# The down projection of a gated feed-forward: eight of 22 tiles as seven block products, three groups of plain tiles around them

## The chip, the cores and the metric
The kernel runs on one core of one Trainium2 chip. A core has five engines with instruction streams of their own: TensorE (PE, matrix products into PSUM), VectorE (DVE), ScalarE (ACT), GpSimd (POOL) and SyncE (SP, which here only starts transfers); they meet through semaphores. Sixteen DMA engines move data between DRAM and the on-chip memory SBUF. The metric is the device time of one execution in microseconds (us); lower is better.

## The reference
A trunk of two layers over 1024 frames and 16 learned meta tokens, model width 1024. Each layer has a mixing half (gated linear attention beside softmax attention, one output projection, residual add) and a gated feed-forward half. Only the second matters here:

```python
def conv_ffn(x, w_up, conv_w, conv_b, w_down):
    h = x @ w_up                              # 1024 -> 2 * 2816
    hp = jnp.pad(h, ((0, 0), (CONV_W - 1, 0), (0, 0)))
    hc = conv_b
    for j in range(CONV_W):                   # causal, 3 taps
        hc = hc + hp[:, j:j + L] * conv_w[j]
    u, g = jnp.split(hc, 2, axis=-1)
    return (jax.nn.silu(g) * u) @ w_down      # 2816 -> 1024
...
        h = h + conv_ffn(rms_norm(h, ffn_norm[i]), w_up[i], conv_w[i], conv_b[i], w_down[i])
    return rms_norm(h, final_norm)[:, N_META:]
```

All is float32, and the output must agree with the reference to nearly that precision.

## The kernel before
Everything is stored transposed: a tile is 128 features (partitions) by up to 1040 tokens. The hidden width 2816 is NFF = 22 such "gated tiles", the model width KD = 8 tiles. A float32 product is made as three products of a rounded type: each operand is split into a rounded high part and the rounded remainder, and `mm3` (lines 212 to 218) accumulates high x high, low x high, high x low in PSUM. ACT makes high parts by a cast, DVE low parts by a subtraction; `split` (line 326) does it for activations, `weights` (line 169) for weights, which SP loads from DRAM into four rotating "raw" buffers.

The up stage (`ffn_up`) makes gated tile j from two output tiles, u and g. It takes them, the two halves of the inner dimension and the two halves of the tokens as a 2 x 2 by 2 x 2 block product and needs seven block products instead of eight (numbered 1 to 7; operands are sums and differences of blocks, several products share a PSUM bank and are taken out of it between them). `up_operand` (line 979) loads and combines the weights, `put` the activations, `evacuate` copies a bank out by ACT (line 1181) or adds it onto a tile by DVE (line 1180). After a tile's last product ACT and DVE apply the convolution (ACT line 1169, DVE line 1173 twice for each of u and g), SiLU and the gate product (line 1202), and POOL starts the write of the tile to `actd[j]` in DRAM (line 1203).

The down stage adds 22 gated tiles times their weights onto the residual. `FGROUPS` cuts the 22 into groups of 5, 5, 5, 4 and 3. `load_act` (line 1228 on) loads a gated tile from `actd` into a slot "st" and splits it into "ah" (ACT, line 330) and "al" (DVE, line 331). While the last up tile runs, the first ten gated tiles are loaded; when a group ends, the next but one is. The first four groups run in `down_tiles`: for each group, for each of the eight output tiles m, all token pieces (three in layer 0, 400, 384 and 256 columns; two of 512 in layer 1, which drops the meta tokens), and DVE adds the PSUM result onto the residual `hT[m]`, which is in SBUF since the start of the stage (line 1249). `stream` asks for the weights of one output tile ahead. The last three gated tiles go to `down_last`, which runs token piece by token piece and feeds the next norm as it goes.

The order of the work is made in two ways. PE's instructions in the feed-forward run as they are written (a manual schedule). On ACT, DVE, POOL and SP a scheduler of the framework orders them by what it expects of their durations, and each stream then runs in that fixed order: an instruction that waits holds up all behind it on its engine. SBUF tiles of 1040 columns are slots of one pool (`self.slots`): `get` takes a free one, `put` gives it back, and the next user of a slot waits for the former one's last reader or writer, transfers among them.

## Time and profile before
| | us |
|---|---|
| median of 3 runs | 2651.08 |
| lowest, highest | 2644.53, 2653.59 |
| the profiled execution | 2645.09 |
| its span, first to last instruction | 2643.3 |
| PE busy in the span | 2523.9 (95%) |
| DVE, ACT, POOL busy | 1759.9 (67%), 1240.1 (47%), 457.9 (17%) |
| mean granted PE clock | 0.987 of full |

The profile is one execution taken by the hardware profiler. Its page gives busy time by engine and the chain of work that ended last; the trace behind it can be asked for waits (who waited for whom), groups of like instructions with counts and mean durations, transfers with their time from issue to landing, timelines, and busy time by stretch of the span. "L217" is line 217 of that kernel; "out<-in" are the names of the tiles. The down stage of layer 0 runs from about 1072 us, that of layer 1 from about 2380 us to the end. A group's busy time counts an instruction from its start to its end; instructions of one engine overlap a little, so the distance between starts is shorter than the duration.

### The profile page before, as it was taken

The numbers are of one execution on the slowest core, as the hardware profiler recorded it, in microseconds if no ns is written. First come the engines' busy times: TensorE is split into PE (matmuls) and PEld (weight loads), VectorE is DVE, ScalarE is ACT, GpSimd is POOL, SyncE is SP. The second block draws the span as 40 slices with busy tenths as digits, with TensorE's granted clock in tenths as the row PEclk, the third lists the DMA queues.
The fourth block names the chain that finished last, engine by engine and source line by source line (L and its number), as shares of the span: only waits on it lengthen the run. The fifth ranks groups of instructions, "written<-read, shape, count | busy, mean of one in ns | idle before, by whom it ended". The sixth has DMA issues, their size and how long they took to land.

```text
span 2643.3 us, 46336 instructions
## 1 busy us (share of the span) xinstructions
PE 2523.9 (95%) x18102; PEld 2407.2 (91%) x18102; DVE 1759.9 (67%) x3484; ACT 1240.1 (47%) x2677; POOL 457.9 (17%) x596
## 2 busy tenths in 40 slices
PE   8999999897999999999999999998989999999997
PEld 7988898897999999999999888887889999998886
DVE  7655676759877777643665666666698767776335
ACT  6345665645544445421343565665455444453112
POOL 4033333333000000000201333332320000000002
PEclk9999999998999999999999999999999999999999
DMA  3222124341222222632312222142512222245222
GB/s 125 65 83 70 47 83 124 106 131 58 97 81 76 85 77 92 217 94 58 103 56 65 75 72 74 56 138 91 158 51 85 83 81 77 83 139 189 65 55 77
DMA packets 114476, 240.72 MB, mean 91 GB/s; under 512 B 14432, under 2 KB 36192, under 8 KB 114256
## 3 DMA queue, kind: packets, MB, share of 16 engines
q1 hardware_dynamic: 96000, 182.27, 22.7%
q0 software_dynamic: 16384, 53.18, 5.5%
q8 instruction: 142, 2.33, 0.4%
q10 hardware_dynamic: 1872, 2.31, 0.2%
q14 instruction: 78, 0.64, 0.1%
HBM read 174.01 MB, written 50.91 MB: 85 GB/s over the span
## 4 chain that ended last, share of the span: by engine, by line
PE 77%; DVE 13%; ACT 4%; issue 3%; DMA 2%; POOL 2%; DVEq 0%; SPq 0%; POOLq 0%; ACTq 0%
PE mm L216 12%; PE mm L217 12%; PE mm L218 12%; PE up L216 10%; PE up L217 10%; PE up L218 10%; PE av L706 2%; PE tr L688 2%; DVE S L655 1%; DVE x L1038 1%; PE wo L217 1%; PE wo L216 1%; PE wo L218 1%; DVE PT L331 1%; ACT P L667 1%
## 5 line engine op out<-in xcount | busy, mean ns | idle before, releaser
L216 PE MATMUL up<-x,hi 128*128 128x260 f32 (+1 forms) x2464 | 701.3, 285 | 22.7 <-DVE hu L1180 20.3
L217 PE MATMUL up<-x,lo 128*128 128x260 f32 (+1 forms) x2464 | 699.2, 284 | 0.0
L218 PE MATMUL up<-x,hi 128*128 128x260 f32 (+1 forms) x2464 | 698.5, 283 | 0.0
L216 PEld LDWEIGHTS up<-x,hi 128*128 128x128 f32 x2464 | 467.5, 190 | 24.4 <-DVE hu L1180 20.7
L217 PEld LDWEIGHTS up<-x,lo 128*128 128x128 f32 x2464 | 467.9, 190 | 0.1
L218 PEld LDWEIGHTS up<-x,hi 128*128 128x128 f32 x2464 | 467.8, 190 | 0.0
L216 PE MATMUL mm<-xh,hi 128*128 128x348 f32 (+4 forms) x1056 | 365.1, 346 | 0.0
L218 PE MATMUL mm<-xl,hi 128*128 128x348 f32 (+4 forms) x1056 | 340.9, 323 | 0.0
L217 PE MATMUL mm<-xh,lo 128*128 128x348 f32 (+4 forms) x1056 | 340.8, 323 | 0.0
L1014 DVE TENSOR_TENSOR lo<-raw,hi 128x512 fp32r<-128x512 f32 x308 | 212.9, 694 | 146.2 <-ACT hi L1013 146.2
L183 ACT CAST hi<-raw 128x512 fp32r<-128x512 f32 (+1 forms) x264 | 142.3, 543 | 329.8 <-PE mm L218 240.0
L217 PE MATMUL mm<-ah,lo 128*128 128x400 f32 (+1 forms) x760 | 266.4, 351 | 0.2 <-DVE lo L185 0.2
L218 PE MATMUL mm<-al,hi 128*128 128x400 f32 (+1 forms) x760 | 265.9, 350 | 0.0
L216 PE MATMUL mm<-ah,hi 128*128 128x400 f32 (+1 forms) x760 | 265.8, 350 | 0.0
L185 DVE TENSOR_TENSOR lo<-raw,hi 128x512 fp32r<-128x512 f32 (+1 forms) x196 | 120.7, 620 | 181.1 <-ACT hi L183 177.5
L1013 ACT CAST hi<-raw 128x512 fp32r<-128x512 f32 x308 | 190.3, 620 | 107.6 <-PE up L218 92.7
L216 PEld LDWEIGHTS mm<-xh,hi 128*128 128x128 f32 x1056 | 201.0, 190 | 6.0 <-issue 5.3
L217 PEld LDWEIGHTS mm<-xh,lo 128*128 128x128 f32 x1056 | 200.9, 190 | 0.4 <-issue 0.3
L218 PEld LDWEIGHTS mm<-xl,hi 128*128 128x128 f32 x1056 | 199.9, 189 | 0.4 <-issue 0.3
L1203 POOL DMA_DIRECT2D actd<-cv x44 | 23.4, 533 | 830.0 <-DVE cv L1202 830.0
L667 ACT ACTIVATE P<-S,m 116x460 f32<-116x460 f32 (+2 forms) x224 | 124.8, 561 | 76.9 <-DVE m L655 72.6
L331 DVE TENSOR_TENSOR PT<-tr,PT 116x464 fp32r<-116x464 f32 (+3 forms) x240 | 122.1, 516 | 55.8 <-ACT PT L330 54.1
(248 smaller groups left out, 5269.0 us busy)
## 6 DMA issues: line engine op xcount, KB each, us to landing
raw<-in_wm_dram SPq DMA_DIRECT2D x328, 256.0 KB, 2.6
raw<-in_wd_dram SPq DMA_DIRECT2D x64, 256.0 KB, 2.6
actd<-cv POOLq DMA_DIRECT2D x22, 520.0 KB, 2.9
st<-actd SPq DMA_DIRECT2D x22, 520.0 KB, 4.9
actd<-cv POOLq DMA_DIRECT2D x22, 512.0 KB, 3.0
st<-actd SPq DMA_DIRECT2D x22, 512.0 KB, 4.8
cb<-cd SPq DMA_DIRECT2D x16, 520.0 KB, 4.2
kA<-kA SPq DMA_DIRECT2D x24, 260.0 KB, 3.8
```

The lines of the kernel that those rows point to most:

```text
L183: nc.scalar.copy(hi[:, :n, :], raw[:, :n, :])
L185: eng.tensor_tensor(out=lo[:, :n, :], in0=raw[:, :n, :], in1=hi[:, :n, :].bitcast(F32), op=ALU.subtract)
L216: nc.tensor.matmul(ps, wh, xh[:, c0:c0 + n], start=first, stop=False, skip_group_check=more)
L217: nc.tensor.matmul(ps, wl, xh[:, c0:c0 + n], start=False, stop=False, skip_group_check=more)
L218: nc.tensor.matmul(ps, wh, xl[:, c0:c0 + n], start=False, stop=last, skip_group_check=more)
L331: nc.vector.tensor_tensor(out=lo, in0=src, in1=hi.bitcast(F32), op=ALU.subtract)
L655: nc.vector.tensor_tensor_reduce(out=S[:rows, :n], in0=S[:rows, :n], in1=cb[:rows, c0:k1], scale=1.0, scalar=(BIG if ci == 0 else m[:rows, ...
L667: nc.scalar.activation(P[:rows, :n], S[:rows, :n], AF.Exp, scale=-1.0, bias=m[:rows, nch - 1:nch], accum_out=(den if nch == 1 else d3[:row ...
L688: nc.tensor.transpose(tr[:w, j, :rows], P[:rows, o:o + w], id_)
L706: nc.tensor.matmul(av[:, a:width], w.rearrange("p a b -> p (a b)"), x, start=(t == 0 and i == 0), stop=(t == last and i == 1))
L1013: nc.scalar.copy(hi[:], src[:])
L1014: nc.vector.tensor_tensor(out=lo[:], in0=src[:], in1=hi[:].bitcast(F32), op=ALU.subtract)
```

## The change
The 22 gated tiles are cut anew: `GROUPS = (("n", 0, 3), ("s", 3, 8), ("r", 11, 4), ("r", 15, 4))` and the last three as before. Lines here are those of the changed kernel.

- Group "n" (tiles 0 to 2) is plain, but its eight results are not added to a residual in SBUF: ACT copies them from PSUM into a slot "do" (line 1414), and POOL starts an accumulating transfer that adds the slot onto `hm[m]`, the residual in DRAM (line 1416). The PSUM tiles are those of the up stage (p0 to p3, two banks each), in token halves of 520 columns (512 in layer 1), each in two pieces of 260 (256).
- Group "s" (tiles 3 to 10) is done by `down_blocks`: output tiles in four pairs, the eight tiles as two halves of four, tokens in two halves; 7 products of 4 inner tiles for each pair. The seven activation operands are made by `prepare` in two sets (inner tiles 0 and 1, then 2 and 3): loads of half tiles, four combinations on DVE and seven splits for each set. Weights are combined and split by `block_operand`, the up stage's function, now with its sources as parameters. Results are built in slots "du" and "dg" by ACT copies and DVE adds and go to `hm` by accumulating transfers too (lines 1348 and 1352).
- Groups "r" are plain and add onto `hT` in SBUF by DVE (line 1412); `hT` is loaded from `hm` only when the first of them begins (line 1393).
- `prepare` is a generator. It yields how many free slots its next step needs, and `pump(n, keep)` runs up to n steps if that many and `keep` more are free. It is called after each product of the last up tile (`tail`), after each plain output tile and within the blocks; `complete` runs what is still missing when a group begins.
- `fetch` asks for the weights of a plain output tile up to two tiles ahead; the first two of group "n" are asked for during the last up tile.

The core of the diff (the weights' functions only gain a parameter `nk`):

```diff
-FGROUPS = [(0, 5), (5, 5), (10, 5), (15, 4), (19, 3)]
+GROUPS, LAST = (("n", 0, 3), ("s", 3, 8), ("r", 11, 4), ("r", 15, 4)), (19, 3)
+HALVES, HALVES_LAST, HALVES_OUT = (0, 520, 520), (8, 524, 516), (16, 528, 512)
-    def down_tiles(self, lyr, hT, pp, o0, dchunks, acts):
...
+    def prepare(self, halves, acts, X):
+        for kind, g0, ng in GROUPS + (("r",) + LAST,):
+            if kind != "s":
+                for j in range(g0, g0 + ng):
+                    yield 3
+                    self.load_act(j, halves[0], acts)
+                continue
...
+                yield 2 + m
+                a0, a1 = load(g0, 0), load(g0, 1)
+                put(1, a0)
+                yield 2 + m
+                b0, b1 = load(g0 + nk, 0), load(g0 + nk, 1)
+                put(2, b0)
+                yield 1 + m
+                tt(a1, b1, a1, ALU.subtract)
+                t2 = get("t2")
+                tt(t2, a1, a0, ALU.add)
+                put(6, t2)
+                yield m
+                tt(a0, b1, t2, ALU.subtract)
+                put(5, a0)
+                s.put(a0)
+                yield m
+                put(7, a1)
+                s.put(a1)
+                yield m
+                tt(b0, b0, t2, ALU.subtract)
+                s.put(t2)
+                put(4, b0)
+                s.put(b0)
+                yield m
+                put(3, b1)
+                s.put(b1)
+    def pump(self, n, keep=3):
+        s = self.slots
+        while n and self.need + keep <= len([i for i in s.free if i not in s.lent]):
+            self.need = next(self.prep)
+            n -= 1
+    def down_blocks(self, lyr, g0, ng, X, pp, fw, halves, after):
...
+        seq = [(0, 1), (0, 2), (1, 1), (0, 6), (0, 5), (0, 7), (0, 4), (0, 3)]
+        for j in range(1, NP):
+            seq += [(j, 2), (j, 6), (j, 5), (j, 7)] + ([(j + 1, 1)] if j + 1 < NP else []) + [(j, 4), (j, 3)]
...
+            elif p == 7:
+                q["g"] = s.get(F32, "dg")
+                copy(q["g"][:, t1])
+                add(q["g"][:, t1], q["x"])
+            elif p == 4:
+                copy(q["g"][:, t0])
+                nc.gpsimd.dma_start(self.hm[2 * j + 1][:, o0:T], q["g"][:, o0:T], accum_op=ALU.add)
+                s.put(q["g"])
+            elif p == 3:
+                add(q["u"][:, t1], q["x"])
+                nc.gpsimd.dma_start(self.hm[2 * j][:, o0:T], q["u"][:, o0:T], accum_op=ALU.add)
+                s.put(q["u"])
...
+    def ffn_down(self, lyr, pp, fw, halves, acts, X, ids):
...
+            out = hT[m] if kind == "r" else s.get(F32, "do")
+            for h in range(2):
+                ps = pp.tile([128, 2, 512], F32, tag=f"p{(2 * m + h) % 4}", name="down", bufs=1)
+                for k in range(ng):
+                    for c in range(2):
+                        self.mm3(ps[:, c, :n], w[k], acts[g0 + k], halves[h] + c * n, n, k == 0, k == ng - 1)
+                x = two(out[:, halves[h]:halves[h] + W])
+                if kind == "r":
+                    nc.vector.tensor_tensor(out=x, in0=ps[:, :, :n], in1=x, op=ALU.add)
+                else:
+                    nc.scalar.copy(x, ps[:, :, :n])
+            if kind == "n":
+                nc.gpsimd.dma_start(self.hm[m][:, o0:T], out[:, o0:T], accum_op=ALU.add)
+                s.put(out)
...
+        def tail(p):
+            self.pump(2 if p == 1 else 1)
+            if p in (5, 7):
+                fetch(parts[0])
-            acts, early = {}, {1: 2, 6: 2, 2: 1, 7: 2, 5: 1, 4: 1, 3: 1}
-            def during_last(p):
-                for _ in range(early[p]):
-                    self.load_act(len(acts), o0, acts)
```

More of the change, by code (lines that the diff above doesn't have):

```diff
@@ L32 @@
 CH_OUT = [(16, 512), (528, 256), (784, 256)]
-CH_DOWN = [(16, 512), (528, 512)]
 CTILES = [(0, 4), (4, 7), (7, 9)]
@@ L46 @@
 V_FIN = DEPTH * NV
-FGROUPS = [(0, 5), (5, 5), (10, 5), (15, 4), (19, 3)]
-HALVES, HALVES_LAST = (0, 520, 520), (8, 524, 516)
+GROUPS, LAST = (("n", 0, 3), ("s", 3, 8), ("r", 11, 4), ("r", 15, 4)), (19, 3)
+HALVES, HALVES_LAST, HALVES_OUT = (0, 520, 520), (8, 524, 516), (16, 528, 512)
 AHEAD = 4
@@ L979, in up_operand, with block_operand @@
     def up_operand(self, lyr, j, p, fw, raws, odd):
-        nc = self.nc
         if j == 2 and p in (1, 2):
             src = fw.tile([128, 4, 128], F32, tag="raw2", name="raw2")
-            nc.sync.dma_start(src[:], self.wm[lyr, M_UP + 4][:, 4 * p - 4:4 * p, :])
+            self.nc.sync.dma_start(src[:], self.wm[lyr, M_UP + 4][:, 4 * p - 4:4 * p, :])
             return self.up_split(src, fw, odd)
+        return self.block_operand(self.wm[lyr, M_UP + 2 * j], self.wm[lyr, M_UP + 2 * j + 1], 4, j, p, fw, raws, odd)
+    def block_operand(self, u, g, nk, j, p, fw, raws, odd):
+        nc = self.nc
         if j not in raws:
-            u, g = self.wm[lyr, M_UP + 2 * j], self.wm[lyr, M_UP + 2 * j + 1]
             q = raws[j] = {}
-            for name, src, k0, own in (("A11", u, 0, True), ("A21", g, 0, False), ("A22", g, 4, False), ("A12", u, 4, True)):
+            for name, src, k0, own in (("A11", u, 0, True), ("A21", g, 0, False), ("A22", g, nk, False), ("A12", u, nk, True)):
                 q[name] = self.wp.tile([128, 4, 128], F32, tag="raw", name="raw", bufs=4) if own else \
                     fw.tile([128, 4, 128], F32, tag="raw2", name="raw2")
-                nc.sync.dma_start(q[name][:], src[:, k0:k0 + 4, :])
+                nc.sync.dma_start(q[name][:, :nk, :], src[:, k0:k0 + nk, :])
         q = raws[j]
@@ L996, in combine @@
                 q[out] = fw.tile([128, 4, 128], F32, tag="raw2", name="raw2")
-            nc.vector.tensor_tensor(out=q[out][:], in0=q[a][:], in1=q[b][:], op=op)
+            nc.vector.tensor_tensor(out=q[out][:, :nk, :], in0=q[a][:, :nk, :], in1=q[b][:, :nk, :], op=op)
         if p == 6:
@@ L1005, in up_operand, with up_split @@
         src = q[{1: "A11", 2: "A12", 3: "A12", 4: "A22", 5: "S1", 6: "S2", 7: "A21"}[p]]
-        return self.up_split(src, fw, odd)
-    def up_split(self, src, fw, odd):
+        return self.up_split(src, fw, odd, nk)
+    def up_split(self, src, fw, odd, nk=4):
         nc = self.nc
@@ L1012, in up_split @@
         lo = pool.tile([128, 4, 128], F32R, tag="lo" + x, name="lo", bufs=3)
-        nc.scalar.copy(hi[:], src[:])
-        nc.vector.tensor_tensor(out=lo[:], in0=src[:], in1=hi[:].bitcast(F32), op=ALU.subtract)
-        return [(hi[:, k, :], lo[:, k, :]) for k in range(4)]
+        nc.scalar.copy(hi[:, :nk, :], src[:, :nk, :])
+        nc.vector.tensor_tensor(out=lo[:, :nk, :], in0=src[:, :nk, :], in1=hi[:, :nk, :].bitcast(F32), op=ALU.subtract)
+        return [(hi[:, k, :], lo[:, k, :]) for k in range(nk)]
     def ffn_up(self, lyr, mix, hT, pp, fw, halves, o0, during_last):
@@ L1238, in load_act, with load, put, tt @@
         acts[j] = (ah, al)
-    def down_tiles(self, lyr, hT, pp, o0, dchunks, acts):
+    def prepare(self, halves, acts, X):
         nc, s = self.nc, self.slots
-        def down(i, m):
-            g0, ng = FGROUPS[i]
-            def f(w):
-                def ev(ps, c0, n):
-                    h = hT[m][:, c0:c0 + n]
-                    nc.vector.tensor_tensor(out=h, in0=ps, in1=h, op=ALU.add)
-                self.dense3(pp, w, [acts[j] for j in range(g0, g0 + ng)], dchunks, ev)
-                if m == KD - 1:
-                    for j in range(g0, g0 + ng):
-                        s.put(*acts.pop(j))
-                    if i + 2 < len(FGROUPS):
-                        a, b = FGROUPS[i + 2]
-                        for j in range(a, a + b):
-                            self.load_act(j, o0, acts)
-            return (self.wd[lyr, m][:, g0:g0 + ng, :], f)
-        return [down(i, m) for i in range(len(FGROUPS) - 1) for m in range(KD)]
+        W = halves[2]
+        for kind, g0, ng in GROUPS + (("r",) + LAST,):
[4 more added lines that the diff above has]
+                continue
+            nk = ng // 2
+            for k0 in range(0, nk, 2):
+                m = min(2, nk - k0)
+                get = lambda name, dt=F32: s.get(dt, name, (128, 2, 520))
+                def load(j, h):
+                    t = get("st")
+                    for i in range(m):
+                        c = halves[h]
+                        nc.sync.dma_start(t[:, i, :W], self.actd[j + k0 + i][:, c:c + W])
+                    return t
+                def put(p, src):
+                    hi = get(f"x{p}", F32R)
+                    lo = get(f"x{p}", F32R) if m == 2 else hi
+                    h, l = (hi[:, :m, :W], lo[:, :m, :W]) if m == 2 else (hi[:, 0:1, :W], hi[:, 1:2, :W])
+                    self.split(h, l, src[:, :m, :W])
+                    X[g0][p].append(([hi, lo] if m == 2 else [hi], h, l))
+                def tt(out, a, b, op):
+                    nc.vector.tensor_tensor(out=out[:, :m, :W], in0=a[:, :m, :W], in1=b[:, :m, :W], op=op)
+                yield 2 + m
[24 more added lines that the diff above has]
+                s.put(b1)
+        yield 99
@@ new lines, in pump, with ensure, evacuate, run @@
+    def pump(self, n, keep=3):
[4 more added lines that the diff above has]
+    def down_blocks(self, lyr, g0, ng, X, pp, fw, halves, after):
+        nc, s = self.nc, self.slots
+        nk, o0, W = ng // 2, halves[0], halves[2]
+        n = W // 2
+        t0, t1 = (slice(c, c + W) for c in halves[:2])
+        two = lambda ap: ap.rearrange("p (a b) -> p a b", b=n)
+        NP = KD // 2
+        seq = [(0, 1), (0, 2), (1, 1), (0, 6), (0, 5), (0, 7), (0, 4), (0, 3)]
+        for j in range(1, NP):
+            seq += [(j, 2), (j, 6), (j, 5), (j, 7)] + ([(j + 1, 1)] if j + 1 < NP else []) + [(j, 4), (j, 3)]
+        raws, ops, st = {}, [], {}
+        wd = lambda m: self.wd[lyr, m][:, g0:g0 + ng, :]
+        def ensure(i):
+            while len(ops) < min(i + 1, len(seq)):
+                j, p = seq[len(ops)]
+                ops.append(self.block_operand(wd(2 * j), wd(2 * j + 1), nk, j, p, fw, raws, len(ops) % 2))
+        def evacuate(j, p):
+            q = st[j]
+            add = lambda out, ps: nc.vector.tensor_tensor(out=two(out), in0=ps[:, :, :n], in1=two(out), op=ALU.add)
+            copy = lambda out: nc.scalar.copy(two(out), q["a"][:, :, :n])
+            if p == 1:
+                q["u"] = s.get(F32, "du")
+                copy(q["u"][:, t0])
+            elif p == 2:
+                add(q["u"][:, t0], q["y"])
+            elif p == 6:
+                copy(q["u"][:, t1])
+            elif p == 7:
[10 more added lines that the diff above has]
+                s.put(q["u"])
+                del st[j]
+        def run():
+            for i, (j, p) in enumerate(seq):
+                ensure(i + AHEAD)
+                q = st.setdefault(j, {})
+                bank, begins = {2: "y", 5: "x", 3: "x"}.get(p, "a"), p in (1, 2, 5)
+                if begins:
+                    place = {1: j % 2, 2: 3, 5: 2}[p]
+                    q[bank] = pp.tile([128, 2, 512], F32, tag=f"p{place}", name="down", bufs=1)
+                ps, w = q[bank], ops[i]
+                ops[i] = None
+                for k in range(nk):
+                    _, hi, lo = X[p][k // 2]
+                    for c in range(2):
+                        self.mm3(ps[:, c, :n], w[k], (hi[:, k % 2, :], lo[:, k % 2, :]), c * n, n,
+                                 begins and k == 0, k == nk - 1, not begins)
+                evacuate(j, p)
+                if j == NP - 1:
+                    for held, _, _ in X.pop(p):
+                        s.put(*held)
+                    if len(ops) == len(seq):
+                        after()
+                    self.pump(1)
+                elif j and p == 5:
+                    self.pump(1, 4)
+        return ensure, run
@@ new lines, in ffn_down, with load_residual, complete, plain @@
+    def ffn_down(self, lyr, pp, fw, halves, acts, X, ids):
+        nc, s = self.nc, self.slots
+        o0, W = halves[0], halves[2]
+        n = W // 2
+        two = lambda ap: ap.rearrange("p (a b) -> p a b", b=n)
+        hT, ahead = [], []
+        def load_residual():
+            for k in range(KD):
+                hT.append(s.get(F32, f"h{k}", first=ids))
+                nc.sync.dma_start(hT[k][:, o0:T], self.hm[k][:, o0:T])
+        def complete(done):
+            while not done():
+                self.need = next(self.prep)
+        def plain(kind, g0, ng, m, w):
+            if m == 0:
+                complete(lambda: all(j in acts for j in range(g0, g0 + ng)))
+                if kind == "r" and not hT:
+                    load_residual()
+            out = hT[m] if kind == "r" else s.get(F32, "do")
+            for h in range(2):
+                ps = pp.tile([128, 2, 512], F32, tag=f"p{(2 * m + h) % 4}", name="down", bufs=1)
+                for k in range(ng):
+                    for c in range(2):
+                        self.mm3(ps[:, c, :n], w[k], acts[g0 + k], halves[h] + c * n, n, k == 0, k == ng - 1)
[7 more added lines that the diff above has]
+                s.put(out)
+            if m == KD - 1:
+                for j in range(g0, g0 + ng):
+                    s.put(*acts.pop(j))
+            self.pump(2)
+        parts = []
+        for kind, g0, ng in GROUPS:
+            if kind == "s":
+                parts.append((g0, ng))
+                continue
+            if not parts or not isinstance(parts[-1], list):
+                parts.append([])
+            parts[-1] += [(kind, g0, ng, m) for m in range(KD)]
+        def fetch(tiles):
+            if len(ahead) < len(tiles):
+                _, g0, ng, m = tiles[len(ahead)]
+                ahead.append(self.weights(self.wd[lyr, m][:, g0:g0 + ng, :]))
+        def run():
+            blocks = None
+            for i, part in enumerate(parts):
+                nxt = parts[i + 1] if i + 1 < len(parts) else None
+                if not isinstance(part, list):
+                    g0, ng = part
+                    complete(lambda: all(len(x) == (ng // 2 + 1) // 2 for x in X[g0].values()))
+                    blocks[1]()
+                    continue
+                if nxt:
+                    then = parts[i + 2] if i + 2 < len(parts) else []
+                    blocks = self.down_blocks(lyr, *nxt, X[nxt[0]], pp, fw, halves,
+                                              lambda t=then: len(ahead) < 2 and fetch(t))
+                for k, t in enumerate(part):
+                    for _ in range(2):
+                        if len(ahead) < k + 3:
+                            fetch(part)
+                    if nxt and k >= len(part) - 2:
+                        blocks[0](2 * (k - len(part) + 2) + 1)
+                    plain(*t, ahead[k])
+                ahead.clear()
+            if not hT:
+                load_residual()
+            complete(lambda: all(j in acts for j in range(LAST[0], sum(LAST))))
+            return hT
+        def tail(p):
+            self.pump(2 if p == 1 else 1)
+            if p in (5, 7):
+                fetch(parts[0])
+        return tail, run
@@ L1261, in down_last @@
     def down_last(self, lyr, hT, pp, dchunks, acts, at_end, es):
         nc, s = self.nc, self.slots
-        g0, ng = FGROUPS[-1]
+        g0, ng = LAST
         w, held = [], []
@@ L1346, in run @@
             dch = CH_OUT if last else CH
-            acts, early = {}, {1: 2, 6: 2, 2: 1, 7: 2, 5: 1, 4: 1, 3: 1}
-            def during_last(p):
-                for _ in range(early[p]):
-                    self.load_act(len(acts), o0, acts)
+            acts, X = {}, {g0: {p: [] for p in range(1, 8)} for kind, g0, _ in GROUPS if kind == "s"}
+            halves = HALVES_OUT if last else HALVES
+            self.prep = self.prepare(halves, acts, X)
+            self.need = next(self.prep)
             with tc.tile_pool(name=f"ffn{lyr}", bufs=1, reuse_waits="tile") as fp, \
@@ L1356, in run @@
                         tc.tile_pool(name=f"up{lyr}", bufs=7, reuse_waits="tile") as fw:
-                    self.ffn_up(lyr, mix, hT, pp, fw, HALVES_LAST if last else HALVES, o0, during_last)
+                    tail, down = self.ffn_down(lyr, pp, fw, halves, acts, X, ids)
+                    self.ffn_up(lyr, mix, hT, pp, fw, HALVES_LAST if last else HALVES, o0, tail)
+                    hT = down()
                 with tc.tile_pool(name=f"dps{lyr}", bufs=8, space=PSUM, reuse_waits="tile") as pp, \
@@ L1360, in run @@
                     ids += s.add(dp, 3 if last else 4, f"d{lyr}_")
-                    hT = [s.get(F32, f"h{k}", first=ids) for k in range(KD)]
-                    for k in range(KD):
-                        nc.sync.dma_start(hT[k][:, o0:T], self.hm[k][:, o0:T])
                     def at_end():
@@ L1372, in at_end @@
                         return n
-                    self.stream(self.down_tiles(lyr, hT, pp, o0, CH_DOWN if last else CH, acts))
                     nm = self.down_last(lyr, hT, pp, dch, acts, at_end, ids)
```

## The prediction
> **What bounds the kernel now.** I read the page's first and fourth part first: which engine is busy, and which one the end hangs on.
> ```profile
> span 2643.3 us, 46336 instructions
> PE 2523.9 (95%) x18102; PEld 2407.2 (91%) x18102; DVE 1759.9 (67%) x3484; ACT 1240.1 (47%) x2677; POOL 457.9 (17%) x596
> PE 77%; DVE 13%; ACT 4%; issue 3%; DMA 2%; POOL 2%; DVEq 0%; SPq 0%; POOLq 0%; ACTq 0%
> ```
> TensorE (PE) is busy 95% of the span and carries 77% of the chain that ended last. Shares over a whole run hide stages, so next come PE's waits: one row for 1060 to 1330 us (layer 0's down stage with its edges) and one for 2365 to 2644 us (layer 1's); the columns after the waiter and the releaser are us in total, times, longest us.
> ```profile
> PE mm L217 <- DVE lo L185: 0.2, 1, 0.2
> PE ssq L316 <- DVE r L305: 2.7, 1, 2.7
> ```
> In the two down stages PE waits for nothing but 0.2 us at the start and 2.7 us in the closing norm. So every matmul taken away there is worth its full interval, and every wait put there costs its full length. The third view is busy time by stretches: the plain groups of layer 0, those of layer 1 without their first matmuls, and a piece of the latter; the columns are PE, weight loads, DVE, ACT, POOL, clock, DMA share, GB/s.
> ```profile
> 1071.76:1288.92 217.16, 216.93 (x1370) 216.62 (x1369) 98.65 (x181) 49.19 (x82) 0.53 (x1) 1.00 0.33 102
> 2381.50:2591.48 209.98, 209.98 (x910) 170.65 (x908) 94.97 (x146) 46.68 (x78) 0.53 (x1) 1.00 0.31 96
> 2488.00:2540.00 52.00, 52.00 (x226) 42.33 (x225) 18.83 (x32) 8.75 (x17) 0.00 (x0) 1.00 0.24 72
> 1060.00:1071.00 11.00, 11.00 (x92) 10.79 (x91) 7.77 (x8) 5.30 (x7) 0.53 (x1) 1.00 1.00 381
> 1071.00:1080.00 9.00, 8.77 (x57) 8.50 (x56) 8.93 (x11) 5.83 (x7) 0.00 (x0) 1.00 1.03 413
> ```
> PE is full, at full clock, while DVE is under half busy. The last two rows are the exception: from 1060 to 1080 us the DMA engines are full (1.00 and 1.03) and DVE is busy 8.93 of 9 us. The change puts its new work exactly there.

> **Matmuls.** Before, groups 1 to 4 hold 19 gated tiles for 8 output tiles: 152 steps of 9 matmuls in layer 0 (216.9 us without the wait) and of 6 in layer 1 (52.00/226 = 0.230 us each; 912 x 0.230 = 209.8 us). After, 11 tiles stay plain (88 steps) and 8 become 4 pairs x 7 products x 4 = 112 half-token steps, worth 56: 144 instead of 152, all in pieces of 260 columns (256 in layer 1). Their interval shows in the up stage, whose tile is 7 products x 24 = 168 matmuls, and in layer 1's last group, from whose first row to the second stand 45 intervals:
> ```profile
> 1022.39 0.53 POOL L1203 DMA_DIRECT2D actd<-cv  x1 [19.61 <-DVE cv L1202]
> 1042.50 0.53 POOL L1203 DMA_DIRECT2D actd<-cv  x1 [19.58 <-DVE cv L1202]
> 1063.80 0.53 POOL L1203 DMA_DIRECT2D actd<-cv  x1 [20.77 <-DVE cv L1202]
> 2608.12 0.28 PE L216 MATMUL mm<-ah,wl 128*128 128x256 f32 x1
> 2613.43 0.28 PE L216 MATMUL mm<-ah,wl 128*128 128x256 f32 x1
> ```
> 20.11/168 = 0.1197 us and 5.31/45 = 0.118 us. Layer 0: 144 x 12 x 0.1197 = 206.8, so -10.1. Layer 1: 1728 x 0.118 = 203.9, so -5.9. Sum -16.0 us, 0.6% of the run: that is all there is to win. A product lasts 24 x 0.1197 = 2.87 us.

> **The first group: DVE.** Three plain tiles now open the stage, 8 x 3 x 12 x 0.1197 = 34.5 us. Under them falls the operand work of the eight block tiles. Its pieces, from the up stage's and the down stage's groups and DVE's timeline at the seam:
> ```profile
> 1061.12 1.23 DVE L331 TENSOR_TENSOR al<-st,ah 128x1040 fp32r<-128x1040 f32 x1
> 1062.27 1.23 DVE L1202 TENSOR_TENSOR cv<-cv 128x1040 f32<-128x1040 f32 x1
> 1065.87 0.70 DVE L1180 TENSOR_TENSOR hg<-up,hg 128x520 f32<-128x520 f32 x1 [0.93 <-ACT hg L1181]
> 1066.49 1.23 DVE L331 TENSOR_TENSOR al<-st,ah 128x1040 fp32r<-128x1040 f32 x1
> L1173 DVE SCALAR_TENSOR_TENSOR cv<-hg,vec,cv 128x1039 f32<-128x1039 f32 x8 | 10.4, 1301 | 3.6 <-ACT cv L1169 3.6
> L330 ACT CAST ah<-st 128x1040 fp32r<-128x1040 f32 x13 | 13.8, 1063 | 21.8 <-DMA st<-actd 20.0 <-DVE al L331 1.8
> L185 DVE TENSOR_TENSOR lo<-raw,hi 128x512 fp32r<-128x512 f32 x32 | 22.0, 690 | 2.8
> ```
> Back to back, a 1040-wide operation advances DVE by 1.15 us (1061.12 to 1062.27) and a 520-wide add by 0.62; the conv step (1.30 busy) I take at 1.21. Two operand sets want 14 residual parts and 8 combinations, 22 x 1.15 = 25 us per layer, where the old groups wanted one residual part per tile (8 x 1.15 = 9). Weight splits fall from 32 to 28 and 16 combinations come in: +12 x 0.6. Averaged over the stage all this fits DVE's idle half; it does not at the seam. By the static order of the changed kernel (E is the end of the last up product), the second pair of loads (actd 7 and 8) takes the slot of up tile 20 and waits for its gate product, which starts the write at about E - 8 (1063.80 against 1071.76). The transfers have these medians from issue to landing:
> ```profile
> raw<-in_wd_dram SPq DMA_DIRECT2D x64, 256.0 KB, 2.6
> actd<-cv POOLq DMA_DIRECT2D x22, 520.0 KB, 2.9
> st<-actd SPq DMA_DIRECT2D x22, 520.0 KB, 4.9
> cb<-cd SPq DMA_DIRECT2D x16, 520.0 KB, 4.2
> h<-hm SPq DMA_DIRECT2D x8, 520.0 KB, 8.5
> ```
> Landing: E - 8 + 4.9 = E - 3.1. Then DVE has in order, ahead of the last up tile's last add, seven 1040-wide operations and one other add, and that add itself: 7 x 1.15 + 2 x 0.62 = 9.3, so it ends at E + 6.2. One of the seven needs ACT's cast x2, whose load is issued only when the write of up tile 20 has landed (E - 8 + 2.9 + 4.9 = E - 0.2), with three casts of 1.06 ahead of it: that adds 0.4, E + 6.6. Output tile 1 needs that bank at E + 4.3 (one tile of 34.5/8): PE waits 2.3. Behind it DVE has four conv steps (4.84), four 1040-wide operations (4.6) and two 384-wide splits (about 0.55 each) before tile 3's weights: E + 17.1 against 3 x 4.3 + 2.3 = 15.3, another 1.8. In layer 1 the order differs by one place (tile 2's split behind the conv chain): 2.2 instead of 1.8. That is 4.1 and 4.5, 8.6 us in both layers. After it DVE stays ahead by about 1 us. ACT, which now takes the first group's sums (16 copies of 0.6) beside 14 casts of 1.06 and the weights' 8, is busy about 29 of 34.5 us: it follows DVE, and costs nothing of its own. The whole chain moves with the landing: at 8.5 us per load (the crowded row) the seam costs 3.6 more per layer, at 2.9 (as the write) 2.0 less. Ends: +4.6 and +15.8; I keep the median load, since the same loads run in the same place now.

> **Adjacent products.** In pairs 0 and 3 product 4 follows product 7 directly, in the same PSUM bank, and may start only when ACT has copied it out. The up stage before has one such hand-over in the timelines of ACT and PE:
> ```profile
> 653.16 0.59 ACT L1181 COPY hu<-up 128x520 f32<-128x520 f32 x1
> 653.80 0.40 PE L216 MATMUL up<-x,hi 128*128 128x260 f32 x1 [1.05 <-ACT hu L1181]
> ```
> PE stood 1.05 us between two products: 4 x 1.05 = +4.2, or 4 x 0.6 = 2.4 if ACT were free at once, more by a cast each (+1.06) if it is not: ends 2.4 and 8.4. Other products of one bank have another one between (2.87 us against a copy of 0.6).

> **Accumulating transfers.** 16 per layer of 0.53 MB replace adds in SBUF. Nothing of before shows one. Bounds on its latency L: the plain write, 2.9, and a write after a read, 2.9 + 4.9 = 7.8. It enters through slots. Plain tile 13's load takes the slot of output tile 1's sum and waits for its accumulate; its cast on ACT stands ahead of the copy that product 7 of pair 1 waits for. From the end of product 4 of pair 0 to that product lie four products, 11.5 us; minus copies, cast and issue (0.6 + 1.0 + 0.6 + 0.2) L and the load's S together may take 9.1 us; pair 3 has the same with tile 16. With DMA at a third in this stage I take L = 5.0 (nearer the middle; an accumulate reads what it writes) and S = 4.2 (the cb load of the same size; the median of st, 4.9, holds the crowded start): 0.1 over, x 4 = +0.4. At 7.8 + 4.9 it is 3.6 x 4 = +14.4; below 9.1 it is 0, never a gain. [...]

> **The rest.** Early weights, the pump and the residual's later load move instructions on SP and POOL. Weights asked two tiles early have 8.6 us between request and use for a transfer of 2.6 and a split of 0.7 on each engine: 0; without that cover each tile would cost up to 2.6. On SP they stand behind the loads that wait for slots, which is why I put those waits into the seam. Of the residual loads moved behind the blocks, tile 7's waits for the last but one accumulate, and on SP the weights of the first r group's tile 3 stand behind it, needed three tiles (3 x 48 x 0.1197 = 17.2 us) after the blocks' end: minus transfer and splits (2.6 + 1.3) and what precedes the issue, free up to L of about 12. POOL's 16 issues x 0.53 = 8.5 us per layer meet a POOL that is busy 0.53 of 217 us. The closing group and norm have the same instructions: 0.

> **Sum.** -16.0 + 8.6 + 4.2 + 0.4 = -2.8 us. The profiled execution took 2645.09 us (span 2643.3); it lies 6.0 under the median of 2651.08. On the median's scale: 2648.3.

> **Rivals.** (1) *The seam does not stall*, because loads land sooner or PE's slips overlap: 8.6 becomes 0 to 3: -8 to -11, 2640 to 2643 as median. For it: loads of two halves of 260 KB, DVE's slack elsewhere. Against: 8.93 of 9 us busy with less work than now. (2) *Slower: the slot chain.* L + S over 9.1 decides, at 4 us for each us; from L + S = 11.8 on (L = 7, S = 4.8) it costs 10.8 instead of 0.4: +7.6, 2659; at 12.7 it is 2662. For it: nothing bounds L closely, and st<-actd has a median of 4.9. Against: DMA share 0.33. (3) *Slower: the first group becomes a DMA stage.* In its 34.5 us fall the operand loads (4.3 MB), eight accumulates (4.3 MB, twice that if the read counts) and weights (2 MB): 10.6 to 14.9 MB; at the 381 to 413 GB/s of the full rows, 26 to 39 us. At the upper end loads take 8.5, and the seam costs 15.8 instead of 8.6, with some slot chain (+4): +8, 2660. [...] (4) *The blocks bring nothing*, since the matmuls stretch to 0.129 us and more when operands move beside them: +16, 2664. Against it stand 168 matmuls in 20.11 us in the up stage, with the same kind of work beside them.

> **How the numbers follow.** A measurement of this kernel can tell about 0.3%, 8 us, from no change. My sum: 0.40, 2648.3, its own range 2640 to 2657. Rival 1: 0.29. Rivals 2 and 3: 0.14 each, 2657 to 2670. Rival 4: 0.03. The sum's case gives 0.03 to faster, rival 1 nothing back: faster 0.32, same 0.37, slower 0.31. The overall one reaches from 2637 (rival 1's 2640 less 3, for the scatter of the runs, 2644.53 to 2653.59) to 2666, inside rivals 2 and 3, whose far ends together (+14.4 + 7.2 over the sum, 2670) I leave out.

> **What would show it.** Right: matmul intervals 0.12 us throughout both stages; PE waits on DVE hu and lo of about 4 us per layer in the first group, four of about 1.0 on ACT's dg, almost none on du. Wrong: waits for du of some us (rival 2), DMA share 1.0 through 35 us and later loads above 8 us (rival 3), no wait on hu (rival 1). What would make the number wrong first is the landing of two loads at E - 3.1.

## The result and the profile after

The changed kernel takes 2665.25 us (median of 5 runs, 2659.5 to 2668.31) against 2651.07 for the kernel before in the same comparison: ratio 1.0055, 95% interval 1.0035 to 1.0074. It is slower by half a percent, where a gain of 0.1% was forecast; the time lies at the upper edge of the range given, on the other side of no change. Its profiled execution took 2667.33 us, 2.1 above its median. The experiments below are given as ratios to runs of the kernel before on the same chip, made beside them, where that kernel took 2646.4 to 2646.8 us; what was expected of e1 to e4 in microseconds goes by the 2651.07 above.

First the page of the changed kernel, the same three parts as quoted of before:
```profile
span 2665.6 us, 48779 instructions
PE 2523.6 (95%) x19278; PEld 2444.0 (92%) x19278; DVE 1796.6 (67%) x3464; ACT 1289.7 (48%) x2745; POOL 485.3 (18%) x628
PE 49%; issue 27%; DVE 13%; ACT 4%; DMA 4%; POOL 3%; DVEq 0%; SPq 0%; POOLq 0%; ACTq 0%
```
PE is busy for as long as before (2523.6 against 2523.9 us), though the down stages hold fewer columns to multiply. PE's waits over the whole run, the rows of tiles named "down" (us in total, times, longest), show where it stood still; the kernel before had 0.2 us in their place:
```profile
PE down L217 <- ACT du L1334: 9.7, 5, 2.3
PE down L217 <- ACT do L1414: 5.4, 2, 3.1
PE down L218 <- DVE lo L186: 3.2, 2, 1.8
PE down L217 <- ACT dg L1334: 3.0, 4, 1.0
PE down L217 <- DVE hu L1184: 1.8, 2, 1.4
```
Next, busy time by stretch, the plain and block groups of both layers (from the first down matmul to the first of the last group), before (layer 1; layer 0's row, 217.16, stands in the prediction) and after, and two stretches of blocks without a stop; columns as in the prediction.
```profile
2380.23:2591.48 211.25, 211.25 (x915) 171.55 (x913) 96.24 (x147) 47.95 (x80) 0.53 (x1) 1.00 0.32 98
```
```profile
1074.37:1299.43 225.06, 213.62 (x1731) 212.14 (x1729) 116.70 (x154) 76.61 (x119) 14.42 (x17) 0.98 0.53 140
2393.24:2612.18 218.94, 207.35 (x1730) 205.71 (x1729) 113.79 (x151) 73.99 (x116) 14.48 (x17) 0.99 0.52 137
1160.00:1190.00 30.00, 30.00 (x252) 30.00 (x252) 15.02 (x20) 11.34 (x19) 3.45 (x4) 1.00 0.55 116
2480.00:2510.00 30.00, 29.99 (x255) 29.78 (x253) 14.25 (x19) 9.53 (x16) 3.23 (x4) 1.00 0.67 154
```
The two stages became 225.06 + 218.94 - 217.16 - 211.25 = 15.6 us longer. (The two profiled executions differ by 22.2; the other 6.6 lie outside the two stages and were not followed up, and the runs of one kernel differ by up to 9.) Where no stop falls, a matmul takes 30/252 = 0.119 and 30/255 = 0.118 us, as the prediction had it, so the saving of 16.0 us is there. It is outweighed by 31.6 us of something else.

What it is can be read from the starts of PE's matmuls. In both stages PE makes 15 stops, and from start to start, less the usual 0.12, they cost 25.5 us: 16.2 at the copies do and du, 5.6 at hu and lo, 3.7 at dg. (From start to start a stop costs 0.16 us more than the wait that the profile names: a matmul lasts 0.28 us where the next one usually starts after 0.12.) After three of the stops (at do, du and lo) the matmuls come at 0.22 us instead of 0.12 for a while: 62 of them, 6.2 us. -16.0 + 25.5 + 6.2 = +15.7. (The matmul after a stop's first comes about 0.1 us late at the other stops too; these terms, some 1.2 us in all, are left out here and in the table below.)

The longest stop, and a later one, seen from ACT (timeline; idle time before an instruction and what ended it in brackets):
```profile
1114.28 1.06 ACT L331 CAST ah<-st 128x1040 fp32r<-128x1040 f32 x1 [7.69 <-DMA st<-actd]
1117.29 1.08 ACT L1414 COPY do<-down 128x520 f32<-128x520 f32 x2
1151.88 1.06 ACT L331 CAST ah<-st 128x1040 fp32r<-128x1040 f32 x1 [5.76 <-DMA st<-actd]
1152.84 0.59 ACT L1334 COPY du<-down 128x520 f32<-128x520 f32 x1
```
The same moments on the two queues that start transfers, and on PE:
```profile
1107.17 0.33 SPq L1238 DMA_DIRECT2D st<-actd  x1
1141.80 0.88 POOL L1348 DMA_DIRECT2D hm<-dg  x1 [22.28 <-DVE lo L1018]
1148.10 0.33 SPq L1238 DMA_DIRECT2D st<-actd  x1
1118.42 0.58 PE L217 MATMUL down<-x,hi 128*128 128x260 f32 x1 [3.13 <-ACT do L1414]
1153.48 0.39 PE L217 MATMUL down<-x,hi 128*128 128x260 f32 x1 [2.31 <-ACT du L1334]
```
ACT is not short of time: it stands idle 7.69 and 5.76 us in front of the cast of a plain tile (11 and 13) that is needed when the blocks end, some 93 and 55 us later, and the copies that PE waits for stand behind that cast in ACT's fixed order. Tile 13's load could start at 1148.10 only, when the accumulate issued at 1141.80 had landed, and its cast could begin at 1151.88: 10.1 us from the one to the other. The other five stops on do and du look alike: ahead of each copy stands a plain tile's cast that waited 4.8 to 8.7 us for its load.

### The profile page after: what moved, and what is told of

Read it like the earlier page. It is cut to its first block, busy times and chain, and to the rows that moved or that the text cites. A ratio compares the mean times of both kernels' runs of the same rounds, so it can differ in the third digit from the quotient of the medians.

```text
span 2665.6 us, 48779 instructions
## 1 busy us (share of the span) xinstructions
PE 2523.6 (95%) x19278; PEld 2444.0 (92%) x19278; DVE 1796.6 (67%) x3464; ACT 1289.7 (48%) x2745; POOL 485.3 (18%) x628
## 2 busy tenths in 40 slices
DMA packets 116790, 257.79 MB, mean 97 GB/s; under 512 B 14688, under 2 KB 32352, under 8 KB 116560
## 4 chain that ended last, share of the span: by engine, by line
PE 49%; issue 27%; DVE 13%; ACT 4%; DMA 4%; POOL 3%; DVEq 0%; SPq 0%; POOLq 0%; ACTq 0%
PE mm L217 7%; PE mm L219 6%; PE mm L218 6%; PE down L217 4%; PE down L219 4%; PE down L218 4%; PE up L217 2%; PE up L218 2%; PE up L219 2%; PE av L707 2%; PE tr L689 2%; DVE S L656 1%; DMA st<-actd 1%; DVE x L1042 1%; PE wo L218 1%
## 5 line engine op out<-in xcount | busy, mean ns | idle before, releaser
L217 PE MATMUL up<-x,hi 128*128 128x260 f32 (+1 forms) x2464 | 700.6, 284 | 22.8 <-DVE hu L1184 20.3
L217 PEld LDWEIGHTS up<-x,hi 128*128 128x128 f32 x2464 | 466.4, 189 | 24.3 <-DVE hu L1184 20.7
L1018 DVE TENSOR_TENSOR lo<-raw,hi 128x512 fp32r<-128x512 f32 x364 | 251.1, 693 | 179.7 <-ACT hi L1017 179.6
L217 PE MATMUL mm<-xh,hi 128*128 128x348 f32 (+4 forms) x1056 | 367.3, 348 | 0.0
L1017 ACT CAST hi<-raw 128x512 fp32r<-128x512 f32 x364 | 224.7, 620 | 134.3 <-PE up L219 92.6
L184 ACT CAST hi<-raw 128x512 fp32r<-128x512 f32 (+2 forms) x200 | 116.7, 587 | 198.3 <-PE down L219 85.2
L217 PEld LDWEIGHTS mm<-xh,hi 128*128 128x128 f32 x1056 | 202.6, 192 | 6.1 <-issue 5.3
L218 PE MATMUL down<-ah,lo 128*128 128x260 f32 (+1 forms) x704 | 198.6, 282 | 3.2 <-DVE lo L186 3.2
L217 PE MATMUL down<-ah,hi 128*128 128x260 f32 (+1 forms) x704 | 199.0, 283 | 1.8 <-DVE hu L1184 1.8
L219 PE MATMUL down<-al,hi 128*128 128x260 f32 (+1 forms) x704 | 198.9, 283 | 0.0
L689 PE MATMUL tr<-ident,P 116*116 116x116 f32 x704 | 129.5, 272 | 25.7 <-DVE PT L332 24.6
## 6 DMA issues: line engine op xcount, KB each, us to landing
raw<-in_wm_dram SPq DMA_DIRECT2D x328, 256.0 KB, 2.6
raw<-in_wd_dram SPq DMA_DIRECT2D x64, 256.0 KB, 3.8
```

The costliest lines, as they stand in the source:

```text
L184: nc.scalar.copy(hi[:, :n, :], raw[:, :n, :])
L217: nc.tensor.matmul(ps, wh, xh[:, c0:c0 + n], start=first, stop=False, skip_group_check=more)
L218: nc.tensor.matmul(ps, wl, xh[:, c0:c0 + n], start=False, stop=False, skip_group_check=more)
L219: nc.tensor.matmul(ps, wh, xl[:, c0:c0 + n], start=False, stop=last, skip_group_check=more)
L689: nc.tensor.transpose(tr[:w, j, :rows], P[:rows, o:o + w], id_)
L1017: nc.scalar.copy(hi[:, :nk, :], src[:, :nk, :])
```

## The experiments

Theory: these stops come from a chain of slots. A sum's slot is free only when its accumulate has landed; a tile loaded into it comes late; ACT, whose order is fixed, waits at that tile's cast, and PE waits for the copy behind it. Rivals: the transfers are late because the DMA engines are crowded, whatever slot they use (their busy share in the first group is 0.82, the last figure but one in the row below); ACT is overloaded; or latency will stop something else wherever the cast stands.
```profile
1074.37:1112.00 37.63, 34.85 (x288) 34.40 (x287) 34.12 (x36) 25.99 (x37) 5.78 (x7) 1.00 0.82 196
```

**Later tiles (e1).** The plain tiles 11 to 18 are not asked for while the first group runs (`self.at`, set in `prepare`, is the kind of group that its next step belongs to).
```diff
-        while n and self.need + keep <= len([...]):
+        while n and (r or self.at != "r") and self.need + keep <= len([...]):
...
-            self.pump(2)
+            self.pump(2, r=kind != "n")
```

> The only change: the plain tiles 11 to 18 are not asked for while the first group runs (its pump stops at the end of the block operands), so their loads come one step later and take slots that were given back longer ago; same matmuls, same transfers, same bytes. Slot theory (the waits on the copies do and du, 15.1 us of the profiled run, and the half-clock spells behind two of them, 4.6 us, come from ACT standing at the cast of a tile whose load waits for an accumulate to land): do and du together under 3 us, the median falls by 14 to 20 us to 2645 to 2651. Rival, crowded transfers (loads are slow because the accumulates fill the DMA engines, whatever slot they take): the load is as late as before and stands before another copy; do and du stay above 10 us, 2660 or more.

Ratio 1.0006 (0.9997 to 1.0016): the loss is gone, 13 us where 14 to 20 were expected. The waits of its PE:
```profile
PE down L218 <- DVE lo L186: 4.7, 3, 1.8
PE down L217 <- ACT du L1336: 4.5, 3, 2.9
PE down L217 <- ACT dg L1336: 3.9, 4, 1.7
```
The waits on do are gone and those on du halved (9.7 to 4.5), though the accumulates take as long (6.0 to 7.3 us for du and do), the loads too (median 5.2 us against 4.9 for the tiles of layer 0), and the same bytes move: slow transfers alone do not make the stops. But 4.5 us is more than the 3 expected; 4.1 of it stands before the last pair, where tile 16's load starts only when an accumulate has just landed (in layer 0 issued at 1178.84, 0.1 us behind it).

**Plain writes (e2).** `accum_op=ALU.add` is left out of all three places, so that the kernel leaves the residual out of its result; it serves for the timing alone.

> Leaves out the adding in all accumulating transfers (they become plain writes of the same tiles, so the residual is lost from the result). Same order, same slots, shorter latency of the transfer (5.3 to 6.7 us against 2.9 for the plain writes of actd). Slot theory: L + S falls from about 11 to about 8, under the 9.1 of the prediction: du waits from 9.7 us to under 2, do from 5.4 to under 3, median 2648 to 2654. A third theory (ACT itself is too slow for casts and copies): du and do stay, 2660 or more.

Ratio 0.9975 (0.9964 to 0.9986), more than expected. Its waits, and the latency of the transfers in the changed kernel and in this one (KB each, median us to landing):
```profile
PE down L217 <- ACT dg L1334: 3.2, 4, 1.0
...
PE down L217 <- ACT du L1334: 0.2, 1, 0.2
```
```profile
hm<-do POOLq DMA_DIRECT2D x8, 520.0 KB, 6.7
hm<-dg POOLq DMA_DIRECT2D x4, 520.0 KB, 5.8
hm<-du POOLq DMA_DIRECT2D x4, 520.0 KB, 6.4
```
```profile
hm<-do POOLq DMA_DIRECT2D x8, 520.0 KB, 3.9
hm<-dg POOLq DMA_DIRECT2D x4, 520.0 KB, 3.2
hm<-du POOLq DMA_DIRECT2D x4, 520.0 KB, 5.2
```
With 1.2 to 2.8 us less per transfer the waits on do and du go from 15.1 to 0.2 us, with every instruction in the same place; those on hu, lo (1.8 and 3.2) and dg stay. ACT is thus not overloaded. What the adding transfer costs more than a plain one makes the 16 us of stops, and with them two of the three slow stretches. Its latency is not all of that: without the add the DMA engines' share in the first group is 0.61 instead of 0.82, and tile 11's load in layer 0 takes 4.5 us instead of 7.0. This run does not tell the two apart.

**Another order of products (e3), and both edits (e4).**
```diff
-        seq = [(0, 1), (0, 2), (1, 1), (0, 6), (0, 5), (0, 7), (0, 4), (0, 3)]
+        seq = [(0, 1), (0, 2), (0, 6), (0, 5), (0, 7), (1, 1), (0, 4), (0, 3)]
...   # last pair: 2 goes from the front to between 7 and 4
+            [(j, 6), (j, 5), (j, 7), (j, 2), (j, 4), (j, 3)]
```

> The order of products in the first and last pair is changed so that another product stands between 7 and 4, nothing else. All theories: the four waits on dg (3.0 us, 3.9 with the restart of PE) go, du and do stay: 2660 to 2663. If the clock spells hang on how much PE stood still within a few us, one of the spells near a dg wait may go or move: a further 2 to 3 us either way.

Ratio 1.0056 (1.0041 to 1.0071), nothing gained, though dg's waits fell from 3.0 to 0.8 us:
```profile
PE down L217 <- ACT du L1335: 10.8, 4, 3.3
...
PE down L217 <- ACT dg L1335: 0.8, 2, 0.4
```

> The first and the third edit together. Slot theory: both gains add up, 2641 to 2648, which would be under the kernel before (2651); what is left of waits is the seam (hu and lo, 5.0 us). Crowding rival: 2657 to 2662.

Ratio 1.0020 (1.0012 to 1.0029): a miss, worse than e1 alone. The gains did not add up. My edit moved product 6 of the first pair one place (2.87 us) nearer to product 1, whose copy it needs; and in both layers ACT stands at a plain tile's cast (7.1 and 8.5 us) ahead of the copy that PE waits for. One place cannot account for a stop of 4.1 us by itself; how much each counts is not shown. The wait of e4 on du, longest of its rows:
```profile
PE down L217 <- ACT du L1337: 7.3, 2, 4.1
```

**Pinned casts (e5).** The order on ACT is changed: the edit pins casts of plain tiles behind everything already written for that engine. The instructions of PE and POOL keep their order; on DVE, and for three weight requests on SP, it shifts a little with ACT's.
```diff
-            nc.scalar.copy(hi, src)
+            c = nc.scalar.copy(hi, src)
+            if pin:
+                self.tc.keep_in_program_order(c)
...
-        self.split(ah[:, o0:T], al[:, o0:T], t[:, o0:T])
+        self.split(ah[:, o0:T], al[:, o0:T], t[:, o0:T], pin=j >= 3)
```

> The casts of plain tiles 11 and up on ACT are pinned behind the copies written ahead of them in the program; loads, slots, transfers and products are those of the changed kernel. Order theory (a slow slot chain costs only because the fixed order of ACT puts the cast of a tile ahead of a copy that PE waits for): the waits on do and du, 15.1 us, fall under 5, the median is 0.998 to 1.001 of the kernel before (the changed one was 1.0055). Rival, latency alone (whatever stands behind a late load waits): the cast now holds up other copies of equal urgency, do, du and dg together stay above 12 us, 1.003 or more.

Ratio 0.9985 (0.9974 to 0.9996): from slower to faster than before by one edit in ACT's order (of the plain tiles only 11 to 21 are pinned, since 3 to 10 are the blocks'). PE's waits, and ACT's waits at these casts in layer 0 for the changed kernel (1068 to 1215 us) and for this one (1076 to 1215 us):
```profile
PE down L218 <- DVE lo L186: 3.2, 2, 1.8
PE down L217 <- ACT dg L1336: 2.7, 4, 0.7
PE down L217 <- DVE hu L1186: 1.1, 1, 1.1
PE down L217 <- ACT du L1336: 0.4, 1, 0.4
```
```profile
ACT ah L331 <- DMA st<-actd: 27.5, 5, 7.9
```
```profile
ACT ah L331 <- DMA st<-actd: 7.8, 2, 7.4
```
Slots and accumulates are those of the changed kernel (6.8, 5.9 and 6.3 us for do, dg and du), the DMA engines' share in the first group is 0.84, and ACT still waits once for 7.4 us, but nothing urgent stands behind it. So neither the latency nor the crowding stops PE by itself: it costs what stands behind the late load on ACT.

**The seam (e6) and all edits together (e8).** Operand steps are held back during the last three products of the up stage: `if p not in (2, 4, 3): self.pump(...)`.

> During the last three products of the up stage no operand steps are issued (the steps for operands 6, 5 and 7 of the first set come after the last up tile's); all else is the changed kernel. Seam theory (hu and lo, 5.0 us, and one half-clock spell of 1.6 come from block operand work ahead of the last up tile's add on DVE): hu and lo together under 2 us, ratio to before 1.0025 to 1.004. Rival: the operands are then late for the first products, and PE waits there instead: 1.005 or more.

Ratio 1.0079 (1.0063 to 1.0095): the rival held. hu is gone and lo down to 0.2 us, and the first group waits for do instead:
```profile
PE down L217 <- ACT do L1414: 14.8, 5, 5.0
...
PE down L218 <- DVE lo L186: 0.2, 1, 0.2
```
ACT then stands at an operand's cast in the middle of the first group, with the copies behind it:
```profile
1095.85 1.06 ACT L331 CAST x<-st 128x1040 fp32r<-128x1040 f32 x1 [6.21 <-DMA st<-actd]
1096.81 0.58 ACT L1414 COPY do<-down 128x520 f32<-128x520 f32 x1
```

> All four edits: waits of the down stages under 3 us together, no half-clock spell: the matmul saving of 16 us is left nearly whole, ratio 0.9935 to 0.996 (2630 to 2637).

Ratio 1.0021 (1.0011 to 1.0030), a miss: 13.8 us of waits on do, the two longest of them (4.0 and 3.5 us) again behind an operand's cast. Of the seam's 5.6 us I have found no way to be rid.

**Versions that beat both.** e7 is e8 without the seam edit; e9 leaves e1's edit out as well, and e10 pins the operands' casts too. Here (1, 2) stands between 7 and 4 of the first pair, so that (1, 1) stays between 1 and 6.

> Late tiles as in the first experiment, pinned casts, and another product between 7 and 4 in the first and last pair, this time without taking the one between 1 and 6 away: do, du and dg together under 1.5 us, seam as before (5 to 6.5): ratio 0.9955 to 0.998.

> The changed kernel with the casts of plain tiles pinned and another product between 7 and 4 in the first and last pair; tiles as early as in the changed kernel, operand steps as in it. If the parts add up: the pinned casts alone left 8.7 us of stops and 1.5 of slow matmuls in the down stages, of which 3.4 are the adjacent products: 5.3 + 1.5 left against 16 saved, ratio 0.996 to 0.998. Rival, the two edits interfere as the first pair of edits did: a new wait on du, 0.999 or more.

> As the one before, with the casts of the block operands pinned too. If these casts also go ahead of copies they should not, the waits on hu and lo at the seam stay (they are DVE's), the rest is as in the one before: 0.996 to 0.998. Rival: pinned operand casts come too late for DVE's split behind them, and the first products wait: 0.999 or more.

Ratios 0.9966 (0.9955 to 0.9977), 0.9968 (0.9955 to 0.9981) and 0.9970 (0.9959 to 0.9981): a third of a percent faster than the kernel before, and not told apart from each other. The ratios are as expected, the waits not all: the profile of e7 (its longest run, 2646.52 us against a median of 2637.38) has 2.3 us on do, where do, du and dg together were to stay under 1.5, and 5.4 on lo; in e10 hu falls to 0.3 us and do takes 1.8. What e9 has left is the seam:
```profile
PE down L218 <- DVE lo L186: 3.2, 2, 1.8
PE down L217 <- DVE hu L1186: 1.5, 2, 1.2
```
The same account as for the changed kernel (-16.0, plus stops from start to start, plus slow matmuls) against the measured change of the two stages, each from one profiled execution:

| kernel | stops | slow | account | stages measured | ratio |
|---|---|---|---|---|---|
| changed | 25.5 | 6.2 | +15.7 | +15.6 | 1.0055 |
| e1 later tiles | 17.1 | 1.8 | +2.9 | +3.0 | 1.0006 |
| e2 plain writes | 9.8 | 1.5 | -4.7 | -4.7 | 0.9975 |
| e3 order of products | 23.8 | 6.3 | +14.1 | +14.1 | 1.0056 |
| e5 pinned casts | 8.7 | 1.5 | -5.8 | -5.5 | 0.9985 |
| e6 seam | 30.7 | 10.1 | +24.8 | +24.0 | 1.0079 |
| e9 pinned, order | 5.3 | 1.6 | -9.1 | -9.9 | 0.9968 |

The account closes to within 1 us in these kernels. Stops, slow matmuls and the length of the stages are all read from the same starts, so this shows only that every other matmul kept its usual interval; what causes a stop is shown by the experiments.

## Why the prediction was wrong

*Matmuls: right.* -16.0 us by intervals of 0.1197 and 0.118; the stretches without a stop show 0.119 and 0.118.

*The seam: right in kind, a third too dear.* 8.6 us forecast at hu and lo, 5.6 measured (and 1.6 of slow matmuls). DVE's queue at the last add is the cause (hu is gone when the work is moved, e6), but that moving it away gains nothing (e6, e8) I had not seen.

*Adjacent products: right.* 4.2 forecast, 3.7 measured; e3 took 2.2 of the 3.0 us of waits away, e9 all.

*Accumulating transfers: the step that failed.* I had the mechanism as it is, the cast of tiles 13 and 16 ahead of a copy, and took L = 5.0 and S = 4.2, 0.1 over a budget of 9.1, for +0.4. The five stops on du cost 10.5 us. For tile 13 in layer 0 L is 6.3 (1141.80 to 1148.10) and S 3.7, together 10.0; for tile 16, and for both in layer 1, L is 5.3 to 5.4 and S 4.9 to 5.4, together 10.4 to 10.9. So L + S was 0.9 to 1.8 us over the budget. The budget itself was too generous: by about 0.2 to 0.4 us in three of the places, and by more at tile 13 in layer 0. There I let the accumulate start 0.8 us after the last product of its sum, and it started at 1141.80, 2.4 us after that product's end at 1139.4 (the product started after dg's stop at 1136.49 and lasts 2.87); the profile names a weight's split on DVE as what released it. 0.9 + 1.6 = 2.5, and PE waited 2.3. The fifth stop (1.9 us, layer 1) stands behind tile 12's cast, which I had not counted. By the medians of layer 0, dg, the accumulate that tiles 13 and 16 wait for, takes 5.8, or 1.8 times the plain write of e2 (3.2); for do it is 1.7 times (6.7 against 3.9) and for du 1.2 (6.4 against 5.2). My 5.0 lay under all three. Its ground, that an accumulate reads what it writes, no run shows apart: the profiles count 257.79 MB with the add and without it.

*"ACT follows DVE, and costs nothing of its own": wrong.* This is the second failed step. I costed the first group's ACT by its busy time, 29 of 34.5 us, and did not look which cast stands last before its last copies: tile 11's, with a load that waits for an accumulate of the same group and then takes 7.0 us in layer 0 and 5.4 in layer 1. That is a part of rival 3, in a milder form: the DMA share in the group is 0.82, not 1.0, and no such load took 8 us. The two stops on do cost 5.7 us in both layers together.

*What no step held: the clock.* 6.2 us of matmuls at half rate after stops (granted clock 0.50 and 0.51 in the rows of the last section), where I had costed a stop at its length.

Rival 2 (slot chain), at 0.14, is what happened in kind. That its price came out so near (10.8 us forecast, 10.5 measured) is partly luck: it asked for L + S of 11.8, and 10.0 to 10.9 sufficed, since the budget was too large and a fifth stop came in. That 2665 lies near its 2659 to 2662 is luck too: the seam cost 3 us less than forecast, and do's 5.7 and the clock's 6.2 stand in no sum of mine. The chances erred in one place: of the two terms that could hardly gain, L was set at 5.0, under the middle of its own bounds (2.9 and 7.8), and ACT at nothing, and the sum of mild values was called the likeliest.

## What to carry to other kernels

A transfer's latency costs by what stands behind its consumer in a fixed order: early loads of data needed 55 to 93 us later cost 16 us here because their casts were put ahead of copies that PE needed within 3, and pinning those casts behind the copies was worth 0.7% (1.0055 to 0.9985). When a change replaces an on-chip add by an accumulating transfer, look up its latency (here 1.2 to 1.8 times that of the plain one) and follow the slot it frees to its next user and that user's place in each engine's queue. And of an engine with spare time ask not how busy it is, but which instruction it may stand at, and who is behind.
